# A decoder layer of three token mixers on one core: row sums of x taken from its transposed blocks, first loads issued behind casts, roots corrected on GpSimd

## The chip, the core and the metric

The kernel runs on one core of one Trainium2 chip. The metric is the device time of one execution in microseconds (us). Before the change the median of three runs is 323.5 us (323.33 to 324.22). The profile shows one execution of the program, taken by the hardware profiler. TensorE is called PE, VectorE DVE, ScalarE ACT, GpSimd POOL and SyncE SP; PEld is PE's weight load.

## What is computed

The input x has 256 rows (tokens) of 1024 float32 values; mem has 256 rows of the same width. In short form, as the reference has it:

```
h = rmsnorm(x, g_in);  z = h @ w_in                  # 8776 columns: q, k, v, gates, logits of three mixers
ya = moba_attention(rope(mq), rope(mk), mv)          # 8 heads of 64, causal
yb = dsa_attention(rope(dq), rope(dk), dv, rope(iq), rope(ik), iw)   # 64 keys chosen by an indexer
yc = cross_attention(xq, *split(rmsnorm(mem, g_mem) @ w_mem_kv))     # 4 heads of 128
u = sum over b of sigmoid(logits_b + b_merge) * ((y_b * silu(gate_b)) @ w_up_b)
out = rmsnorm(x + u @ w_out, g_final)
```

rmsnorm divides each row by the root of its mean square plus 1e-6. That factor of x (x_rstd) and of mem (m_rstd), one number per row, is what the change computes in another way.

## The kernel before, in words

**Products.** Every float32 matrix is split into a high part (a cast to fp32r on ACT) and a low part (the difference, on DVE), and a product is three matmuls: high x high, high x low, low x high. x and mem come transposed (xT, memT: 1024 features as 8 blocks of 128 partitions, 256 tokens each), are multiplied by g_in or g_mem while they are split (`split_act`, lines 180 to 191), and stay in SBUF. The row factors are applied after the product, where results leave PSUM.

**Steps.** All weights are cut into 100 steps of up to 512 KB (`plan.steps`); the list ORDER and the helpers `gemm...` set their order. Steps 0 to 7 take mv and mq in turn (mv's blocks 0 and 1, mq's 0 and 1, mv's 2 and 3, and so on), so that two steps use up one pair of xT's blocks. Then mk0, mk1, the indexer's i0, and the rest. The main loop (lines 984 to 1004) issues, for step s: the split of a pair of x's blocks (first four even steps), side work that was hung on s, the load of step s+6 (`load_weights`), the split of step s+3 (`split_weights`), the first half of the products of s, side work of s + 0.5, and the second half. Negative s is the run-up.

**What sets the order.** On PE and GpSimd the instructions stand in the order in which the program issues them. On DVE, ACT and SP the framework orders them, by program order as priority and by when it expects inputs and buffers to be free; `tc.issue_after(i)` keeps an instruction of the same engine behind i. A DMA is issued by SP or, where `queue=nc.scalar` is given, by ACT. Raw weights have four buffers (WRAW), so a load waits for the low part of the step four before it; split weights have five.

**The start.** SP issues x_first (xT's block 0 with gains and biases), w0's first block, xT's block 1, w0's second block, w1 in two halves, xT's blocks 2 and 3 and w2 (lines 171 to 175 and 969 to 973). `load_late` (lines 975 to 982) issues w3 and xT's blocks 4 and 5 on ACT behind the last cast of w0, and w4, w5 and xT's blocks 6 and 7 on SP. Meanwhile PE runs nine warm-up products of 128x128 (WARM, line 967).

**Roots.** `load_rows` (lines 887 to 892) loads x a second time, not transposed, in two loads of 128 rows (LOAD_ROWS = -2). `start_stats` (line 894, hung on step 6) squares the rows on ACT with an accumulated sum, and `rsqrt` (line 214) makes x_rstd: a scaling on DVE, a square root on ACT, a reciprocal and a Newton correction of four small operations on DVE (lines 220 to 223, 128x2 each). From x_rstd come `tab`, `rB` (its transposed form, two PE transposes at step 8, line 913) and all results scaled by row. For mem, `square_sum` (line 193) squares each pair of transposed blocks on ACT and adds the pairs up on DVE, and `row_sums` (line 203) sums over partitions with products with a column of ones; m_rstd and its transposes mB follow at steps 21.5 and 23.5. MEM gives the steps at which mem's four pairs are loaded (2, 7, 11, 15); each is split three steps later. xT's raw blocks and memT's share one buffer.

**Attention.** `attend` hangs each pair of heads of mixer A on two steps given in M_PAIRS: at s0 the scores (`self_scores`: PE, then a masked minimum on DVE, exponentials on ACT), half a step later their scaling on GpSimd (`self_scale`, line 616), at s1 the transposes of the probabilities (`self_transpose`: PE, a cast mph on ACT, the difference mpl on DVE), a step later the product with v (`self_values`, line 642, output mya). `idx_transpose` (line 443) turns the indexer's queries at steps 27 and 28 through PSUM banks of the kind "sc", of which there are two, used by scores too.

Of the kernel before, what the change touches and what calls it, by code (L numbers as in the profile page):

```python
# [58 lines left out]
SPLIT_AHEAD = 3  # L59
LOAD_AHEAD = 6  # L60
WRAW = 4
WARM = 9
HALVED = 2
ORDER = (
# [4 lines left out]
)  # L69
LOAD_ROWS = -2  # L70
X_STATS = 6

IDX = (27, 29, 33.5)

TURNS = (('mq', 8.5, 15.5), ('mk', 13.5, 20.5), ('dq', 27, 30), ('dk', 34, 37.5))

M_PAIRS = ((23, 25.5), (24, 27.5), (26.5, 29.5), (29.5, 31.5))
D_PAIRS = ((43.5, 47.5), (47.5, 49), (52, 53.5), (54.5, 55.5))
X_HEADS = (41.5, 44.5, 49, 50.5)
GATES = 59.5  # L80

MEM = (2, 7, 11, 15, 21.5)


def block_places(blocks, nk):
# [8 lines left out]
class Steps:  # L94
# [11 lines left out]
    def at(self, step, fn, *args):  # L106
        self.side[step].append((fn, args))
# [3 lines left out]
def hybrid_layer_kernel(  # L111
# [14 lines left out]
    nc = tc.nc  # L126
# [3 lines left out]
    work = ctx.enter_context(tc.tile_pool(name="work", bufs=2))  # L130
# [6 lines left out]
    at = plan.at  # L137
# [22 lines left out]
    acts = {}  # L160
# [19 lines left out]
    def split_act(raw, hi, lo, gcol, pair, nm):  # L180
        for j in range(2):
            k = 2 * pair + j
            g = x_first[:, S + gcol + k : S + gcol + k + 1]
            src = x_first[:, 0:S] if nm == "x" and k == 0 else raw[:, j, :]
            nc.scalar.activation(hi[:, k, :], src, AF.Copy, scale=g)
            nc.vector.scalar_tensor_tensor(
                lo[:, k, :], src, g, hi[:, k, :].bitcast(F32),
                op0=OP.mult, op1=OP.subtract,
            )
        if nm == "e":  # L190
            square_sum(raw, nm, pair)

    def square_sum(raw, nm, pair):

        sq = work.tile([P, 2, S], F32, name=f"{nm}sq{pair}", tag=("nat" if pair == 0 else "gate"),
                       bufs=3)
        nc.scalar.activation(sq, raw, AF.Square)
        if pair == 0:
            acts[nm, "sq"] = sq
        else:  # L200
            nc.vector.tensor_tensor(acts[nm, "sq"], acts[nm, "sq"], sq, op=OP.add)

    def row_sums(nm):

        ps = psum.tile([P, 512], F32, name=f"{nm}ss", tag="tp", bufs=1)
        for t in range(2):
            for j in range(2):
                nc.tensor.matmul(
                    ps[:, t : t + 1], acts[nm, "sq"][:, j, t * P : (t + 1) * P], ones[:, 0:1],
                    start=j == 0, stop=j == 1,  # L210
                )
        return ps[:, 0:2]

    def rsqrt(r, ss, nm):

        v, sd, e = (work.tile([P, 2], F32, name=f"{nm}n{i}", tag=f"n{i}") for i in range(3))
        nc.vector.tensor_scalar(v, ss, 1.0 / D, EPS, op0=OP.mult, op1=OP.add)
        nc.scalar.activation(sd, v, AF.Sqrt)
        nc.vector.reciprocal(r, sd)
        nc.vector.tensor_tensor(e, r, r, op=OP.mult)  # L220
        nc.vector.tensor_tensor(e, e, v, op=OP.mult)
        nc.vector.tensor_scalar(e, e, -0.5, 1.5, op0=OP.mult, op1=OP.add)
        nc.vector.tensor_tensor(r, r, e, op=OP.mult)


    loaded, halves = {}, {}
    last_hi = [None]

    def load_weights(s, j=None, queue=nc.sync):
        src, off, nk_all, n, k0, nk = plan.steps[s][0]  # L230
        if not j:
            loaded[s] = raws.tile([P, nk, n], F32, name=f"w{s}r", tag="wraw", bufs=WRAW)
        a, b = (0, nk) if j is None else (j, j + 1)
        v = bass.AP(
            tensor=src.tensor, offset=src.offset + off + (k0 + a) * n,
            ap=[[nk_all * n, P], [1, (b - a) * n]],
        )
        queue.dma_start(loaded[s][:, a:b, :].rearrange("p k n -> p (k n)"), v)

    def split_weights(s):  # L240
        raw = loaded.pop(s)
        shape = list(raw.shape)
        hi = ws.tile(shape, F32R, name=f"w{s}h", tag="whi")
        lo = ws.tile(shape, F32R, name=f"w{s}l", tag="wlo")
        part = 1 if s < HALVED + 2 else shape[1]
        for j in range(0, shape[1], part):
            ks = slice(j, j + part)
            last_hi[0] = nc.scalar.copy(hi[:, ks, :], raw[:, ks, :]).ins
            nc.vector.tensor_sub(lo[:, ks, :], raw[:, ks, :], hi[:, ks, :].bitcast(F32))
        halves[s] = (hi, lo)  # L250

# [191 lines left out]
    def idx_transpose(t):  # L443
# [4 lines left out]
                idx[nm] = keep.tile([P, 3 * P], F32, name=nm, tag=nm)  # L448
        tok = slice(t * P, (t + 1) * P)
        for j in range(2):  # L450
            tp = psum.tile([P, 4, P], F32R, name=f"iqt{t}{j}", tag="sc", bufs=2)
            for g in range(4):
                nc.tensor.transpose(tp[:, g, :], idx["qs", t][:, 4 * j + g, :], ident_r)
            nc.scalar.copy(idx["q"][j][:, :, tok], tp)
# [427 lines left out]
    attend("m", M_PAIRS, lambda: bias_c)  # L882
    attend("d", D_PAIRS, lambda: idx["sel"])

    x_rows = []

    def load_rows():
        for t in range(2):
            rows = keep.tile([P, 4, S], F32, name=f"x_rows{t}", tag=("khi", "klo")[t])
            rows = rows.rearrange("p a b -> p (a b)")  # L890
            nc.sync.dma_start(rows, x[t * P : (t + 1) * P, :])
            x_rows.append(rows)

    def start_stats():
        sums = work.tile([P, 2], F32, name="xss", tag="xss", bufs=1)
        for t in range(2):
            junk = work.tile([P, D], F32, name=f"xjunk{t}", tag="sw", bufs=1)
            nc.scalar.activation(junk, x_rows[t], AF.Square, accum_out=sums[:, t : t + 1])
        rsqrt(x_rstd, sums, "x")
        nc.vector.tensor_scalar_mul(xs_rstd, x_rstd, float(P**-0.5))  # L900
        nc.vector.tensor_copy(ident_r, ident)
        for t in range(2):
            nc.vector.tensor_scalar_mul(tab[:, t, :], tab0[:, t, :], x_rstd[:, t : t + 1])
# [11 lines left out]
            )  # L915
        nc.vector.tensor_copy(dst, tp[:, 0:S])

    at(LOAD_ROWS, load_rows)
    at(X_STATS, start_stats)
    at(X_STATS, make_bias)  # L920
    at(X_STATS + 2, rstd_rows, x_rstd, rB, "rB")
# [44 lines left out]
    warm = psum.tile([P, 512], F32, name="warm", tag="tp", bufs=1)  # L966
    for _ in range(WARM):
        nc.tensor.matmul(warm[:, 0:P], ones, ones, start=True, stop=True)  # L968
    first = [load_act(xT, 0, "x", 0)]
    load_weights(1, 0)  # L970
    load_weights(1, 1)
    first.append(load_act(xT, 0, "x", 1))
    load_weights(2)

    def load_late():

        with tc.issue_after(last_hi[0]):
# [91 lines left out]
```

## Time and profile before

| what | value |
|---|---|
| median of three runs | 323.5 us (323.33 to 324.22) |
| the profiled execution's own time | 324.77 us |
| its span, from the first to the last instruction | 323.0 us |
| moved by DMA | 59.45 MB, 184 GB/s over the span |

The profile counts as busy the time in which an engine has an instruction in it; matmuls are pipelined, so PE's busy share is high where matmuls follow each other, and its holes are what is to be looked for. In the timeline a row gives the start, the duration, engine, line, operation, output and inputs by the program's names, the shapes, how many were merged, and in brackets the idle time of the engine just before and what ended it. Lines such as L249 are lines of the kernel. A letter q behind an engine's name (SPq, ACTq) marks its sequencer, which issues DMAs.

### The profile page before, as it was taken

How to read it: one execution, taken by the hardware profiler on the slowest of the kernel's cores; microseconds unless marked ns; L12 is line 12 of the kernel's file. 1: busy time of each engine (PE TensorE's matmuls, PEld its weight loads, DVE VectorE, ACT ScalarE, POOL GpSimd, SP SyncE). 2: the span in 40 equal slices, each digit the busy share in tenths (PEclk: the TensorE clock that was granted, in tenths of full speed). 3: DMA queues.
4: the chain of work that ended last, by engine and by line, in shares of the span. 5: the costliest groups of instructions: out<-in, count | busy, mean ns of one | idle time of the engine just before them, and what ended most of it. 6: DMA issues, size and time to landing. Idle time of an engine off the chain costs nothing.

```text
span 323.0 us, 6395 instructions
## 1 busy us (share of the span) xinstructions
PE 313.0 (97%) x2442; PEld 297.4 (92%) x2442; DVE 252.1 (78%) x458; ACT 202.9 (63%) x357; POOL 41.9 (13%) x58
## 2 busy tenths in 40 slices
PE   8899999998999999999999999999999999999992
PEld 7699999988999989879999999999999999998882
DVE  3579999899799999988766759998466775677523
ACT  5599674687878545577666588756444546643434
POOL 0001000017202000010200235321000111014011
PEclk9999999999999999999999999999999999999999
DMA  6989886864644446574443434478765666655003
GB/s 202 379 293 333 269 269 194 265 240 124 214 130 127 138 130 210 182 246 131 146 132 117 146 94 162 136 220 302 211 193 189 190 188 205 182 156 188 2 0 130
DMA packets 18368, 59.45 MB, mean 184 GB/s; under 512 B 2209, under 2 KB 2465, under 8 KB 18337
## 3 DMA queue, kind: packets, MB, share of 16 engines
q1 hardware_dynamic: 17760, 57.73, 57.1%
q10 hardware_dynamic: 576, 1.31, 1.0%
q8 instruction: 19, 0.31, 0.5%
q14 instruction: 13, 0.10, 0.1%
HBM read 55.89 MB, written 1.05 MB: 176 GB/s over the span
## 4 chain that ended last, share of the span: by engine, by line
PE 70%; DVE 15%; DMA 5%; ACT 4%; issue 4%; SPq 0%; ACTq 0%; DVEq 0%
DMA w3r<-w_in 3%; DVE wk L498 2%; DMA w25r<-w_in 2%; DVE m L496 1%; PE o_0ps L255 1%; PE o_0ps L256 1%; PE o_0ps L254 1%; DMA w0r<-w_in 1%; PE dya L642 1%; PE i_0ps L280 1%; PE i_1ps L280 1%; PE mv_1ps L280 1%; PE mv_0ps L280 1%; DVE acc L487 1%; PE lg L480 1%
## 5 line engine op out<-in xcount | busy, mean ns | idle before, releaser
L747 POOL TENSOR_TENSOR u<-u,gt 128x512 f32<-128x512 f32 x7 | 9.9, 1411 | 76.7 <-DVE gt L744 76.7
L616 POOL TENSOR_SCALAR dpr<-dpr,dst 128x128 f32<-128x128 f32 (+1 forms) x16 | 6.6, 425 | 84.1 <-DVE dst L614 83.9
L616 POOL TENSOR_SCALAR mpr<-mpr,mst 128x128 f32<-128x128 f32 (+1 forms) x16 | 9.8, 629 | 56.3 <-DVE mst L614 56.3
L734 ACT ACTIVATE gt<-gt,x_first 128x256 f32<-128x256 f32 x24 | 10.9, 501 | 2.7 <-DVE gt L731 2.5
L606 ACT ACTIVATE dpr<-dms,dst 128x128 f32<-128x128 f32 (+1 forms) x16 | 7.1, 446 | 3.6 <-DVE dst L602 3.6
L788 ACT ACTIVATE junk<-xn 128x512 f32<-128x512 f32 (+1 forms) x5 | 2.7, 543 | 8.6 <-DVE xn L786 8.6
L606 ACT ACTIVATE mpr<-mms,mst 128x128 f32<-128x128 f32 (+1 forms) x16 | 7.1, 444 | 1.2 <-DVE mst L602 1.2
L664 ACT ACTIVATE xpr<-xsc,xst,xs_rstd 128x256 f32<-128x256 f32 x8 | 4.4, 560 | 3.4 <-DVE xst L660 3.4
L752 ACT CAST us<-u 128x512 fp32r<-128x512 f32 x4 | 2.5, 624 | 6.2 <-POOL u L747 4.9
L647 ACT COPY dyT<-dya 64x256 f32<-64x256 f32 x8 | 2.9, 367 | 4.2 <-PE dya L642 4.1
L484 ACT ACTIVATE rl<-lg 128x384 f32<-128x384 f32 x8 | 3.9, 485 | 2.7 <-PE lg L480 1.6
L487 DVE SCALAR_TENSOR_TENSOR acc<-rl,iw,acc 128x128 f32<-128x128 f32 (+1 forms) x14 | 5.4, 431 | 0.1
L480 PE MATMUL lg<-ikT,iqT 128*128 128x128 f32 (+1 forms) x32 | 5.1, 282 | 0.1
L968 PE MATMUL warm<-ones 128*128 128x128 f32 x18 | 4.0, 419 | 1.1 <-DVE eps_t L963 1.1
L602 DVE CUSTOM_DVE_ANT_0 mms<-msc,bias_c 128x128 f32<-128x128 f32 (+1 forms) x16 | 5.0, 350 | 0.0
L968 PEld LDWEIGHTS warm<-ones 128*128 128x128 f32 x18 | 3.9, 328 | 1.1 <-DVE eps_t L963 1.1
L648 DVE TENSOR_TENSOR dyT<-dyT,dya 64x256 f32<-64x256 f32 x8 | 3.3, 417 | 1.8 <-ACT dyT L647 1.7
L628 ACT CAST dph<-dtp 128x384 fp32r<-128x384 f32 x8 | 3.8, 479 | 1.4 <-PE dtp L627 1.3
L629 DVE TENSOR_TENSOR dpl<-dtp,dph 128x384 fp32r<-128x384 f32 x8 | 4.4, 553 | 0.4
L602 DVE CUSTOM_DVE_ANT_0 dms<-dsc,sel 128x128 f32<-128x128 f32 (+1 forms) x16 | 4.7, 352 | 0.0
L786 DVE TENSOR_TENSOR xn<-o_0ps,xn 128x512 f32<-128x512 f32 x2 | 1.4, 691 | 4.2 <-PE o_0ps L256 4.2
L498 DVE MATCH_REPLACE8 wk<-m,wk 128x128 f32<-128x128 f32 (+1 forms) x14 | 4.7, 342 | 0.0
(1296 smaller groups left out, 1541.9 us busy)
## 6 DMA issues: line engine op xcount, KB each, us to landing
x_rows<-x SPq DMA_DIRECT2D x2, 512.0 KB, 8.7
eT<-memT SPq DMA_DIRECT2D x4, 256.0 KB, 4.6
xn<-x SPq DMA_DIRECT2D x2, 512.0 KB, 5.5
w0r<-w_in SPq DMA_DIRECT2D x2, 256.0 KB, 3.3
w1r<-w_in SPq DMA_DIRECT2D x2, 256.0 KB, 4.9
xT<-xT SPq DMA_DIRECT2D x2, 256.0 KB, 7.1
w2r<-w_in SPq DMA_DIRECT2D x1, 512.0 KB, 7.3
w3r<-w_in ACTq DMA_DIRECT2D x1, 512.0 KB, 8.7
```

What stands on the lines that cost most here:

```text
L280: nc.tensor.matmul(accs[nm][t][:, :n], a[p](k, slice(t * P, (t + 1) * P)), w[q][:, half, :], start=k + i == 0, stop=k + i == nk + 1,)
L480: nc.tensor.matmul(lg[:, c : c + n], q[:, q0:q1], idx["k"][:, j, 0:n], start=j == 0, stop=j == 1)
L487: nc.vector.scalar_tensor_tensor(acc[:, c], rl[:, c], iw[:, t, g : g + 1], (bias_c if g == 0 else acc)[:, c], op0=OP.mult, op1=OP.add,)
L498: nc.vector.match_replace(out=wk[:, c], in_to_replace=m8[t], in_values=src[:, c], imm_value=TAKEN)
L602: nc.vector.tensor_tensor_reduce(out=ms[:, c], in0=sc[:, c], in1=bias()[:, c], op0=OP.add, op1=OP.min, scale=-(HD**-0.5), scalar=3e38, acc ...
L606: big["last_exp"] = nc.scalar.activation(pr[:, c], ms[:, c], AF.Exp, bias=st[:, t : t + 1], scale=-1.0, accum_out=st[:, 2 + t : 3 + t],)
L616: nc.gpsimd.tensor_scalar(pr[:, c], pr[:, c], st[:, 4 + t : 5 + t], 1.0, op0=OP.mult, op1=OP.mult)
L629: nc.vector.tensor_sub(pl, tp[:, 0 : 3 * P], ph.bitcast(F32))
L664: big["last_exp"] = nc.scalar.activation(pr3[:, t, :], sc[:, t, :], AF.Exp, bias=st[:, t : t + 1], scale=xs_rstd[:, t : t + 1], accum_out= ...
L734: nc.scalar.activation(gt[:, f, :], gt[:, f, :], AF.Sigmoid, bias=x_first[:, j : j + 1])
L747: adder.tensor_tensor(u, u, gt, op=OP.add)
L968: nc.tensor.matmul(warm[:, 0:P], ones, ones, start=True, stop=True)
```

## The change

- **Row sums of x.** The second load of x and the squares over its rows are gone. `square_sum` now also runs for x, on its four pairs of transposed blocks, at steps 1, 2, 3 and 4 (X_SQUARES), and folds the two blocks of the pair sum into one at the end, so that `row_sums` needs one product per 128 tokens instead of two, for x and for mem. x's row sums stand at step 6.
- **Loads.** `load_late` is called twice, behind each cast of w1's two halves: first xT's third pair and then w3 on ACT, then w4 on ACT, w5 on SP and behind it xT's last pair. The two tables cst and tabT are kept behind the last load that was issued before step 1.
- **First cast.** The first cast of w0 is done in two halves of its columns, one on ACT and one on DVE.
- **Roots.** The four correcting operations of `rsqrt` run on GpSimd.
- **Places.** One warm-up product less; the second pair of mixer A at step 24.5 instead of 24; mem's first pair loaded at step 5 instead of 2; the transposes of the indexer's queries go through PSUM banks of the kind "mm", of which there are four.

```
-WARM = 9
+WARM = 8
-LOAD_ROWS = -2
+X_SQUARES = (1, 2, 3, 4)
-M_PAIRS = ((23, 25.5), (24, 27.5), (26.5, 29.5), (29.5, 31.5))
+M_PAIRS = ((23, 25.5), (24.5, 27.5), (26.5, 29.5), (29.5, 31.5))
-MEM = (2, 7, 11, 15, 21.5)
+MEM = (5, 7, 11, 15, 21.5)
...
-        nc.scalar.activation(sq, raw, AF.Square)
+        raw = acts[nm, "raw"]
+        if nm == "x" and pair == 0:
+            nc.scalar.activation(sq[:, 0, :], x_first[:, 0:S], AF.Square)
+            nc.scalar.activation(sq[:, 1, :], raw[:, 1, :], AF.Square)
+        else:
+            nc.scalar.activation(sq, raw[:, 2 * pair : 2 * pair + 2, :], AF.Square)
         if pair == 0:
             acts[nm, "sq"] = sq
-        else:
-            nc.vector.tensor_tensor(acts[nm, "sq"], acts[nm, "sq"], sq, op=OP.add)
+            return
+        total = acts[nm, "sq"]
+        nc.vector.tensor_tensor(total, total, sq, op=OP.add)
+        if pair == 3:
+            nc.vector.tensor_tensor(total[:, 0, :], total[:, 0, :], total[:, 1, :], op=OP.add)
...
-            for j in range(2):
-                nc.tensor.matmul(
-                    ps[:, t : t + 1], acts[nm, "sq"][:, j, t * P : (t + 1) * P], ones[:, 0:1],
-                    start=j == 0, stop=j == 1,
-                )
+            nc.tensor.matmul(
+                ps[:, t : t + 1], acts[nm, "sq"][:, 0, t * P : (t + 1) * P], ones[:, 0:1],
+                start=True, stop=True,
+            )
...
-        nc.vector.tensor_tensor(e, r, r, op=OP.mult)
-        nc.vector.tensor_tensor(e, e, v, op=OP.mult)
-        nc.vector.tensor_scalar(e, e, -0.5, 1.5, op0=OP.mult, op1=OP.add)
-        nc.vector.tensor_tensor(r, r, e, op=OP.mult)
+        nc.gpsimd.tensor_tensor(e, r, r, op=OP.mult)
+        nc.gpsimd.tensor_tensor(e, e, v, op=OP.mult)
+        nc.gpsimd.tensor_scalar(e, e, -0.5, 1.5, op0=OP.mult, op1=OP.add)
+        nc.gpsimd.tensor_tensor(r, r, e, op=OP.mult)
...
-            last_hi[0] = nc.scalar.copy(hi[:, ks, :], raw[:, ks, :]).ins
+            cols = slice(0, shape[2] // 2 if s + j == 0 else shape[2])
+            last_hi[0] = nc.scalar.copy(hi[:, ks, cols], raw[:, ks, cols]).ins
+            if s + j == 0:
+                cols = slice(shape[2] // 2, shape[2])
+                nc.vector.tensor_copy(hi[:, ks, cols], raw[:, ks, cols])
+            if s == 1:
+                load_late(j)
...
-            tp = psum.tile([P, 4, P], F32R, name=f"iqt{t}{j}", tag="sc", bufs=2)
+            tp = psum.tile([P, 4, P], F32R, name=f"iqt{t}{j}", tag="mm", bufs=4)
...
-        sums = work.tile([P, 2], F32, name="xss", tag="xss", bufs=1)
-        for t in range(2):
-            junk = work.tile([P, D], F32, name=f"xjunk{t}", tag="sw", bufs=1)
-            nc.scalar.activation(junk, x_rows[t], AF.Square, accum_out=sums[:, t : t + 1])
-        rsqrt(x_rstd, sums, "x")
+        rsqrt(x_rstd, row_sums("x"), "x")
...
-    at(LOAD_ROWS, load_rows)
+    for pair, s0 in enumerate(X_SQUARES):
+        at(s0, square_sum, "x", pair)
...
-    def load_late():
+    def load_late(j):
         with tc.issue_after(last_hi[0]):
-            load_weights(3, queue=nc.scalar)
-            first.append(load_act(xT, 0, "x", 2, nc.scalar))
-        load_weights(4)
-        load_weights(5)
-        first.append(load_act(xT, 0, "x", 3))
+            if j == 0:
+                first.append(load_act(xT, 0, "x", 2, nc.scalar))
+                load_weights(3, queue=nc.scalar)
+            else:
+                load_weights(4, queue=nc.scalar)
+                load_weights(5)
+                with tc.issue_after(last_load[0]):
+                    first.append(load_act(xT, 0, "x", 3))
...
+        if s == 1:
+            mark = last_load[:]
         if s == 4:
-            nc.sync.dma_start(cst, consts[:, 0:512])
-            nc.sync.dma_start(tabT.rearrange("p t c -> p (t c)"), consts[:, 512:1024])
+            with tc.issue_after(mark[0]):
+                nc.sync.dma_start(cst, consts[:, 0:512])
+                nc.sync.dma_start(tabT.rearrange("p t c -> p (t c)"), consts[:, 512:1024])
```

## Rows read from the trace of the kernel before

**Rows 1.** The page: busy time of each engine, and the granted clock in 40 slices.
```profile
PE 313.0 (97%) x2442; PEld 297.4 (92%) x2442; DVE 252.1 (78%) x458; ACT 202.9 (63%) x357; POOL 41.9 (13%) x58
...
PEclk9999999999999999999999999999999999999999
```

**Rows 2.** Busy time by stretch: length, busy us of each engine, clock, DMA share, GB/s.
```profile
2.00:9.00 7.00, 6.79 (x31) 5.51 (x30) 2.96 (x5) 3.41 (x8) 0.00 (x0) 1.00 0.85 265
...
5.01:18.74 13.73, 12.82 (x72) 10.01 (x72) 8.46 (x14) 8.25 (x16) 0.00 (x0) 1.00 0.98 356
18.74:61.90 43.16, 43.16 (x343) 42.08 (x342) 39.99 (x64) 31.44 (x50) 1.25 (x2) 1.00 0.84 263
30.00:60.00 30.00, 30.00 (x255) 30.00 (x255) 29.09 (x44) 19.55 (x33) 0.00 (x0) 1.00 0.80 239
61.90:80.00 18.10, 16.69 (x141) 15.29 (x141) 17.58 (x54) 14.68 (x33) 6.74 (x11) 1.00 0.59 191
```

**Rows 3.** PE's waits: line, whom it waited for, us in total, times, longest.
```profile
PE mya L642 <- DVE mpl L629: 1.0, 1, 1.0
PE mBt L913 <- DVE m_rstd L223: 0.4, 1, 0.4
```

**Rows 4.** PE's timeline at the start: warm-up, first products of steps 0, 1, 4, 6.
```profile
1.05 4.05 PE L968 MATMUL warm<-ones 128*128 128x128 f32 x18 [1.05 <-DVE eps_t L963]
...
5.01 0.50 PE L280 MATMUL mv_0ps<-w0h,xhi 128*128 128x512 f32 x1
...
8.18 0.29 PE L254 MATMUL mq_0ps<-xhi,w1h 128*128 128x256 f32 x1
...
18.86 0.40 PE L280 MATMUL mv_0ps<-w4h,xhi 128*128 128x512 f32 x1
...
24.45 0.40 PE L280 MATMUL mv_0ps<-w6h,xhi 128*128 128x512 f32 x1
```

**Rows 5.** ACT's timeline at the start: casts of weights and the issue of w3.
```profile
4.34 0.62 ACT L248 CAST w0h<-w0r 128x512 fp32r<-128x512 f32 x1 [0.89 <-DMA w0r<-w_in]
...
6.05 1.31 ACTq L238 DMA_DIRECT2D w3r<-w_in  x1
7.41 0.62 ACT L248 CAST w1h<-w1r 128x512 fp32r<-128x512 f32 x1 [1.17 <-DMA w1r<-w_in]
...
11.32 1.14 ACT L248 CAST w2h<-w2r 128x512 fp32r<-128x512 f32 x2 [0.58 <-DMA w2r<-w_in]
14.76 1.14 ACT L248 CAST w3h<-w3r 128x512 fp32r<-128x512 f32 x2 [2.30 <-DMA w3r<-w_in]
```

**Rows 6.** The page's DMA issues: tile, count, KB each, median us from issue to landing.
```profile
x_rows<-x SPq DMA_DIRECT2D x2, 512.0 KB, 8.7
```

**Rows 7.** Instructions grouped by line and shape: busy us, mean ns of one, idle before.
```profile
L898 ACT ACTIVATE xjunk<-x_rows 128x1024 f32<-128x1024 f32 x2 | 2.1, 1052 | 0.0
...
L516 ACT COPY mqT<-mq_0ps 128x256 f32<-128x256 f32 x2 | 0.7, 372 | 0.0
...
L201 DVE TENSOR_TENSOR esq<-esq,esq 128x512 f32<-128x512 f32 x3 | 2.0, 678 | 0.0
```

**Rows 8.** Timeline: first and last step of mem's root on DVE; x's transposes on PE.
```profile
63.81 0.17 DVE L219 RECIPROCAL m_rstd<-en 128x2 f32<-128x2 f32 x1 [0.32 <-ACT en L218]
...
66.92 0.15 DVE L223 TENSOR_TENSOR m_rstd<-m_rstd,en 128x2 f32<-128x2 f32 x1
...
30.05 0.38 PE L913 MATMUL rBt<-cst,x_rstd 128*128 128x128 f32 x2
```

**Rows 9.** GpSimd's scalings of 128x128: two from 75.1 us, one from 69 us.
```profile
L616 POOL TENSOR_SCALAR mpr<-mpr,mst 128x128 f32<-128x128 f32 x2 | 2.8, 1422 | 0.0
...
L616 POOL TENSOR_SCALAR mpr<-mpr,mst 128x128 f32<-128x128 f32 x1 | 0.4, 372 | 40.4 <-DVE mst L614 40.4
```

**Rows 10.** Timeline: the cast before mpl on ACT, the second pair's scalings on GpSimd.
```profile
75.98 0.46 ACT L628 CAST mph<-mtp 128x384 fp32r<-128x384 f32 x1
...
75.02 5.53 POOL L616 TENSOR_SCALAR mpr<-mpr,mst 128x128 f32<-128x128 f32 x6
```

More of the change, by code (lines that the diff above doesn't have):

```diff
@@ L190, in split_act, with square_sum @@
         if nm == "e":
-            square_sum(raw, nm, pair)
-    def square_sum(raw, nm, pair):
+            square_sum(nm, pair)
+    def square_sum(nm, pair):
         sq = work.tile([P, 2, S], F32, name=f"{nm}sq{pair}", tag=("nat" if pair == 0 else "gate"),
                        bufs=3)
-        nc.scalar.activation(sq, raw, AF.Square)
+        raw = acts[nm, "raw"]
[4 more added lines that the diff above has]
+            nc.scalar.activation(sq, raw[:, 2 * pair : 2 * pair + 2, :], AF.Square)
         if pair == 0:
             acts[nm, "sq"] = sq
-        else:
-            nc.vector.tensor_tensor(acts[nm, "sq"], acts[nm, "sq"], sq, op=OP.add)
+            return
[3 more added lines that the diff above has]
+            nc.vector.tensor_tensor(total[:, 0, :], total[:, 0, :], total[:, 1, :], op=OP.add)
     def row_sums(nm):
@@ L219, in rsqrt @@
         nc.vector.reciprocal(r, sd)
-        nc.vector.tensor_tensor(e, r, r, op=OP.mult)
-        nc.vector.tensor_tensor(e, e, v, op=OP.mult)
-        nc.vector.tensor_scalar(e, e, -0.5, 1.5, op0=OP.mult, op1=OP.add)
-        nc.vector.tensor_tensor(r, r, e, op=OP.mult)
+        nc.gpsimd.tensor_tensor(e, r, r, op=OP.mult)
+        nc.gpsimd.tensor_tensor(e, e, v, op=OP.mult)
+        nc.gpsimd.tensor_scalar(e, e, -0.5, 1.5, op0=OP.mult, op1=OP.add)
+        nc.gpsimd.tensor_tensor(r, r, e, op=OP.mult)
     loaded, halves = {}, {}
-    last_hi = [None]
+    last_hi, last_load = [None], [None]
     def load_weights(s, j=None, queue=nc.sync):
@@ L237, in load_weights @@
         )
-        queue.dma_start(loaded[s][:, a:b, :].rearrange("p k n -> p (k n)"), v)
+        last_load[0] = queue.dma_start(
+            loaded[s][:, a:b, :].rearrange("p k n -> p (k n)"), v
+        ).ins
     def split_weights(s):
@@ L883, in hybrid_layer_kernel @@
     attend("d", D_PAIRS, lambda: idx["sel"])
-    x_rows = []
-    def load_rows():
-        for t in range(2):
[L889 to L892, printed above, removed]
-    def start_stats():
-        sums = work.tile([P, 2], F32, name="xss", tag="xss", bufs=1)
-        for t in range(2):
-            junk = work.tile([P, D], F32, name=f"xjunk{t}", tag="sw", bufs=1)
-            nc.scalar.activation(junk, x_rows[t], AF.Square, accum_out=sums[:, t : t + 1])
-        rsqrt(x_rstd, sums, "x")
+    def start_stats():
+        rsqrt(x_rstd, row_sums("x"), "x")
         nc.vector.tensor_scalar_mul(xs_rstd, x_rstd, float(P**-0.5))
@@ L959, in hybrid_layer_kernel @@
     at(end["u01"], load_tail)
+    first = [load_act(xT, 0, "x", 0)]
     nc.vector.memset(ones, 1.0)
@@ L968, in hybrid_layer_kernel @@
         nc.tensor.matmul(warm[:, 0:P], ones, ones, start=True, stop=True)
-    first = [load_act(xT, 0, "x", 0)]
     load_weights(1, 0)
@@ L996, in hybrid_layer_kernel @@
             split_weights(s + SPLIT_AHEAD)
-            if s + SPLIT_AHEAD == 0:
-                load_late()
         if s >= 0:
```

## The prediction

> **What bounds the kernel now.** I read the page first: TensorE (PE) is busy 97% of the span and VectorE (DVE) 78%, GpSimd (POOL) 13%; the granted clock is full in all 40 slices, that is 2.4 GHz [rows 1], so the clock is no term of the sum. A busy PE is not an unbroken PE, so next came the table by stretch [rows 2]. Between 18.74 and 61.90 us PE is busy for all of 43.16 us; there only less matmul work would help, and the change removes none. What can be won lies where PE has holes: from 5.01 to 18.74 us, where the 16 DMA engines are 98% busy, and from 61.90 to 80 us, where DVE is busy 17.58 of 18.10 us. The list of PE's waits [rows 3] names the two that make the second stretch's 1.41 idle us: 0.97 for the first pair's probabilities (mpl) and 0.44 for the memory's root (m_rstd).
>
> The start is read from PE's timeline [rows 4]. Undisturbed, two steps take 24.45 - 18.86 = 5.59 us, 2.80 each. Steps 1 to 3 take 18.86 - 8.18 = 10.68 us, where 8.39 would do: 2.29 us are lost. Their cause stands in ScalarE's (ACT) timeline [rows 5]: the casts wait for w1r, w2r and w3r. w3r is issued at 6.05 and cast only at 14.76, because xT's third part, w4, two loads of x's rows and w5 are issued around it and share the same engines; the loads of x's rows take 8.7 us each to land [rows 6].
>
> **First product.** It starts at 5.01 [rows 4], when the cast of w0's first block ends (4.34 + 0.62 [rows 5]); the warm-up ends there too (4.05 us from 1.05 [rows 4]). The change splits the cast: a 128x256 copy takes 0.37 on ACT [rows 7], so it ends at about 4.72; one warm-up product of nine less takes 0.45 off. The start moves by about 0.26. Step 0's second block waits for its own load as now, and its order of products leaves room for an end 0.26 earlier. Term: **-0.26 us**; bounds 0 and -0.45.
>
> **Loads behind casts, x's rows gone.** Two loads of 512 KB leave the queue [rows 6], at 356 GB/s [rows 2] 2.9 us of all the DMA engines, and two issues leave SP. xT's third part and w3 are now issued behind w1's first cast, so at 7.0 to 7.4 instead of up to 6.05, w4 behind its second cast, w5 and xT's last part after that on SP. What must land before step 2 (x_first, w0, two parts of xT, w1, w2) is 2.07 MB by shape; at 265 GB/s, the rate of 2 to 9 us [rows 2], it is there at about 9.7 if nothing shares; w2 is cast at 11.32 now. w3 makes it 2.84 MB, at 356 GB/s 2.2 us later: 12 to 13 with some sharing, and PE asks for it at about 14. So w3 stops being late. What is late next is ACT: three issues stand between its casts, and w3r's issue held it for 1.31 us [rows 5], so w1's second cast would start near 8.7, no earlier than now, and the lo parts still come one DVE operation later. I leave 0.9 of the 2.29 us: **-1.4 us**; bounds -0.3 (each issue takes 1.31, and step 2 starts hardly earlier) and -2.29 (the issues hold nothing).
>
> **Row sums from the blocks.** Out go two squares over whole rows, 2 x 1.05 us of ACT [rows 7] between 18 and 21 us; in come three squares of 128x512 at 0.62 (the cast of that size, [rows 5]) and one in two halves of 0.37, 2.6 us, at steps 1 to 4. DVE gets three sums of 0.68 [rows 7], two folds and a copy of half that size (0.4 each, an estimate from it): 3.2 us, while eight small operations of 0.15 [rows 8] leave it. Most lies before 20 us, where DVE is busy 8.46 of 13.73 us [rows 2]; without that cover it would be 2 us more in the chain of rival 1. On PE the sums of x cost what those of mem save, as each needs half the products. But x's sums now stand in PE's order at step 6, at 24.45 - 1.66 = 22.8. The last block of x, loaded behind w5, I expect squared by 19 and folded by 20.5: no wait. Term: **0**; bounds 0 and +0.5.
>
> **Roots on GpSimd.** The memory's root takes from 63.81 to 67.07 on DVE [rows 8], since each 0.15 us step gets its turn behind a subtraction of 1.2 us, and PE waits 0.44 for it. No two-input GpSimd operation on two columns is in the trace. The nearest rows are 128x128 scalings, of which one took 0.37 and two 1.42 each where DVE ran w28l to w30l [rows 9]. Four operations would take 1.5 to 5.7 us, against 3.26. DVE's order now would let two of them meet w25l and w26l and two meet operations that read PSUM: about 3.1. Term: **-0.1 us**; bounds -0.44 and the loss of rival 2. For x the reciprocal comes at best at 23.8 (sums 0.4, root and reciprocal 0.6), the four end at 26.9, and PE transposes them at step 8, 30.05 - 1.66 + 0.4 = 28.8 [rows 8]: covered.
>
> The Trainium skill (SBUF — State Buffer, Who interferes with whom) says that a VectorE instruction with two SBUF inputs and a GpSimd instruction that reads SBUF shut each other out for a whole instruction. By that rule the 1.42 beside 0.37 is this lock, the trace agrees, and the sum would be rival 2's.
>
> **Second pair half a step later.** PE waits 0.97 us in mya [rows 3], because ACT casts mph only at 75.98 [rows 10], behind the second pair's exponentials. Half a step is 1.4 us. If the pair falls behind mph, mpl is there in time and the wait goes; if the order on ACT and DVE stays, nothing does. The pair's own scalings end at 80.5 [rows 10] and its transposes come at step 27.5, after 83 us, so a loss is excluded. Between 0 and -0.97 I take **-0.5 us**.
>
> The rest costs nothing. mem's first part is issued three steps later, and its buffer is x's, so it waits for x's last reader now too; three weight loads pass it on SP. The tables cst and tabT may go out right after w6, 0.5 MB that nothing near needs to wait for. The transposes of iq move to another bank; none of PE's seven waits is theirs.
>
> Sum: -0.26 - 1.4 - 0 - 0.1 - 0.5 = **-2.26 us**. The profiled execution took 324.77 (span 323.0), 1.27 above the median of 323.5; less 2.26 it would be 322.5, and the median 321.2. The 1.66 us of the first two terms are kept from 18.86 to 61.9, where PE has no hole, if DVE keeps pace.
>
> **Rivals.**
> 1. **DVE gives it back.** Between 30 and 60 us DVE is busy 29.09 of 30 us [rows 2]. If that chain doesn't start earlier, PE arrives 1.66 us earlier at m_rstd and mpl and waits as much longer; only 0.2 is left: 323.3. Against it: the chain hangs on casts that hang on the same late loads, and 2.1 us of ACT leave just ahead of it.
> 2. **GpSimd's four steps each wait out a DVE operation** (the other side). At 1.42 each, from 62.3 (63.98 - 1.66), m_rstd is there at 68.0; PE asks now at about 66.7, then at 65.0, and waits 3.0 us instead of 0.44. x's root ends at 23.8 + 5.7 = 29.5 for 28.8: 0.7 more. 2.5 + 0.7 - 1.66 = +1.6, the pair unmoved: 325.1. It makes the kernel slower by over 0.3% from 1.35 us per step on. For it: the rows of 1.42 [rows 9]. Against: the row of 0.37, and a 128x2 operation is shorter.
> 3. **Both late waits go and no load is late**: -0.26 - 2.29 - 0.44 - 0.97 = -3.96: 319.5.
> 4. **It doesn't do what it says**: the order on DVE, ACT and SP is the framework's. If x's last block comes late, PE waits at step 6; if the issues hold ACT, the second term is -0.3: 322.3 to 323.
>
> **How the numbers follow.** Forecast 0.50, rival 1 0.16, rival 2 0.11, rival 3 0.17, rival 4 0.06. The likeliest time is 321.2, its own range 320.2 to 322.4. About 0.3% (0.97 us) is what a measurement of this kernel can tell from no change. Faster by more (under 322.53): the forecast, rival 3 and most of rival 4, 0.71; within it: rival 1 and the rest of 4, 0.18; slower: 0.11. The range reaches to rival 3's time and just past rival 1's, 319.3 to 323.6, and leaves out rival 2 and little below.
>
> **What would show it.** Right: PE's first product at about 4.75, step 4 at 17.2 instead of 18.86, no wait for w3r, m_rstd some 3 us after its reciprocal, a shorter wait in mya. Wrong: w1's second cast held by issues on ACT; GpSimd operations on two columns of over 1 us; a longer wait at mBt, or a new one at rBt or for x's sums; waits at 62 to 80 us that grow by what the start won.

## The result, and the profile after

The changed kernel takes 327.96 us (median of four executions, 327.7 to 330.25), the kernel before beside it 323.41 (322.72 to 324.22): a ratio of 1.0135, 95% interval 1.0098 to 1.0173. It is slower, by 4.55 us; the forecast was 321.2 and its range ended at 323.6. The profiled executions are 2.9 us apart (327.7 and 324.77; spans 325.9 and 323.0), since the one of before lay 1.4 above its median and the one after 0.3 below. The traces explain these 2.9.

The page of the changed kernel, against [rows 1]: shares alike, and the clock full in all slices but the last of 40.

```profile
PE 316.8 (97%) x2440; PEld 302.6 (93%) x2440; DVE 254.3 (78%) x456; ACT 203.0 (62%) x358; POOL 45.5 (14%) x66
...
PEclk9999999999999999999999999999999999999998
```

By stretch (length, busy us of each engine, clock, DMA share, GB/s), against [rows 2]: the DMA engines are a little freer at the start, and VectorE is as full as before from 30 to 60 us.

```profile
5.01:18.74 13.73, 13.26 (x75) 10.75 (x76) 9.71 (x16) 9.98 (x19) 0.00 (x0) 1.00 0.93 324
30.00:60.00 30.00, 30.00 (x251) 30.00 (x250) 29.54 (x47) 19.51 (x34) 0.24 (x2) 1.00 0.73 221
```

PE's waits (line, whom it waited for, us in total, times, longest), against [rows 3]: m_rstd is gone, mya shorter, and a small one is new, at x's sums (xss); xpt, mv_0ps and the indexer's product lg (0.1 before) wait 0.1 to 0.2 longer. By this list the change worked.

```profile
PE mya L657 <- DVE mpl L644: 0.6, 1, 0.6
PE xpt L699 <- ACT xpr L689: 0.5, 1, 0.5
PE mv_0ps L295 <- ACT w2h L258: 0.4, 1, 0.4
PE lg L495 <- DVE mst L617: 0.2, 1, 0.2
PE xss L215 <- DVE xsq L209: 0.2, 1, 0.2
```

The start of PE's timeline (start, duration), against [rows 4], then ACT's, against [rows 5]:

```profile
1.05 3.78 PE L972 MATMUL warm<-ones 128*128 128x128 f32 x16 [1.05 <-DVE eps_t L967]
4.91 0.74 PE L295 MATMUL mv_0ps<-w0h,xhi 128*128 128x512 f32 x1
...
8.64 0.28 PE L269 MATMUL mq_0ps<-xhi,w1h 128*128 128x256 f32 x1
...
18.10 0.40 PE L295 MATMUL mv_0ps<-w4h,xhi 128*128 128x512 f32 x1
...
24.12 0.58 PE L215 MATMUL xss<-ones,xsq 128*128 128x1 f32 x4 [0.24 <-DVE xsq L209]
24.55 0.48 PE L295 MATMUL mv_0ps<-w6h,xhi 128*128 128x512 f32 x1
```

```profile
4.45 0.41 ACT L258 CAST w0h<-w0r 128x256 fp32r<-128x256 f32 x1 [0.68 <-DMA w0r<-w_in]
...
6.21 0.62 ACT L258 CAST w0h<-w0r 128x512 fp32r<-128x512 f32 x1 [0.57 <-DMA w0r<-w_in]
...
7.26 0.44 ACTq L245 DMA_DIRECT2D w3r<-w_in  x1
8.73 0.62 ACT L258 CAST w1h<-w1r 128x512 fp32r<-128x512 f32 x1 [1.28 <-DMA w1r<-w_in]
...
11.42 1.14 ACT L258 CAST w2h<-w2r 128x512 fp32r<-128x512 f32 x2 [0.61 <-DMA w2r<-w_in]
13.29 1.14 ACT L258 CAST w3h<-w3r 128x512 fp32r<-128x512 f32 x2 [0.73 <-DMA w3r<-w_in]
```

Step 4 starts at 18.10, 0.76 earlier than before, where 1.66 was forecast: w3's wait is down from 2.30 to 0.73, and its issue took 0.44, not 1.31, but w0's second block, w1 and w2 are still waited for. Step 6 is 0.10 later than before: PE reaches x's sums at 23.88 and waits for VectorE's fold, which stands behind w7's subtraction (VectorE's timeline):

```profile
22.41 1.23 DVE L264 TENSOR_TENSOR w7l<-w7r,w7h 128x1024 fp32r<-128x1024 f32 x1
23.55 0.42 DVE L209 TENSOR_TENSOR xsq<-xsq 128x256 f32<-128x256 f32 x1
```

Where the 2.9 us come from shows only when steps are timed from first product to first product. Step 30 starts at 96.75 before and 96.45 after (-0.30); from there to step 92 it is 197.60 and 201.28 (+3.68); the rest is 28.61 and 28.17 (-0.44). Between 30 and 92 the waits hardly differ (0.24 more at xpt, 0.11 less at dya); most products start later after the one ahead of them. The first products of steps 60 and 70, a stretch without a wait, before and then after:

```profile
204.75 0.28 PE L254 MATMUL l00ps<-xhi,w60h 128*128 128x256 f32 x1
...
232.75 0.28 PE L254 MATMUL u01ps<-mgyh,w70h 128*128 128x256 f32 x1
```

```profile
205.57 0.28 PE L269 MATMUL l00ps<-xhi,w60h 128*128 128x256 f32 x1
...
234.37 0.28 PE L269 MATMUL u01ps<-mgyh,w70h 128*128 128x256 f32 x1
```

Ten steps of 24 products of 256 columns take 28.00 us before and 28.80 after: 116.7 and 120.0 ns a product. The row's duration, 0.28 in both, doesn't show this. Products of 512 columns went the other way, 233.3 to 226.7 ns (steps 36 to 37).

### The profile page after: what moved, and what is told of

It is laid out like the page before. It is cut to its first block, busy times and chain, and to the rows that moved or that the text cites. A ratio compares the mean times of both kernels' runs of the same rounds, so it can differ in the third digit from the quotient of the medians.

```text
span 325.9 us, 6401 instructions
## 1 busy us (share of the span) xinstructions
PE 316.8 (97%) x2440; PEld 302.6 (93%) x2440; DVE 254.3 (78%) x456; ACT 203.0 (62%) x358; POOL 45.5 (14%) x66
## 4 chain that ended last, share of the span: by engine, by line
PE 69%; DVE 15%; DMA 6%; issue 3%; ACT 3%; POOL 2%; SPq 0%; ACTq 0%; DVEq 0%
DMA w3r<-w_in 2%; DMA w7r<-w_in 2%; PE i_0ps L295 2%; PE i_1ps L295 2%; POOL mpr L631 1%; DVE wk L513 1%; DMA w0r<-w_in 1%; PE o_0ps L270 1%; PE o_0ps L269 1%; PE o_0ps L271 1%; DVE m L511 1%; PE dya L657 1%; DMA w42r<-w_kv 1%; PE dtp L642 1%; PE o_1ps L271 1%
## 5 line engine op out<-in xcount | busy, mean ns | idle before, releaser
L631 POOL TENSOR_SCALAR dpr<-dpr,dst 128x128 f32<-128x128 f32 (+1 forms) x16 | 7.6, 490 | 85.2 <-DVE dst L629 84.7
L807 POOL TENSOR_TENSOR xn<-xn,gf 128x512 f32<-128x512 f32 x2 | 2.6, 1296 | 15.7 <-ACT junk L803 15.7
```

Source lines behind the costliest of these rows:

```text
L631: nc.gpsimd.tensor_scalar(pr[:, c], pr[:, c], st[:, 4 + t : 5 + t], 1.0, op0=OP.mult, op1=OP.mult)
```

## The experiments

**What sets the rate.** The clock is the same. What differs for every product is where its operands lie. The change drops the tile xss, 32 bytes a partition, from a pool that is laid out ahead of x, mem and all later operands, while the weights' halves stay: in the compiled program x's high part lies at byte 138272 of a partition before and 138240 after, w0's at 52224 in both. Three runs put a tile back or add one, and only the size ([P, 2] is 32 bytes, [P, 16] is 64) and the kernel differ; a fourth repeats the changed kernel as it is:

```
     def start_stats():
+        pad = work.tile([P, 2], F32, name="pad", tag="pad", bufs=1)
+        nc.gpsimd.memset(pad, 0.0)
```

> The changed kernel with a tile of two columns (32 bytes a partition in the pool) put back where x's sums (xss) had stood, and one GpSimd memset of it, so that x, mem and all that lies behind them in SBUF stand again at an odd multiple of 32 bytes. Theory (addresses): PE's products of 256 columns start 116.7 ns after each other again and those of 512 columns 233.3 ns, steps take 2.80 us; 1823 products of 256 columns get 3.33 ns each back (6.1 us), 216 of 512 columns lose 6.6 ns each (1.4 us): 4.6 us less, about 323.3 us. Rival A (the order of PE's instructions, or the PSUM banks): 120 and 226.7 ns stay, 327.9 us. Rival B (that chip on that day): this kernel and the changed one unaltered come out alike, whatever the rate.

> The kernel before with the same tile of 32 bytes added, so that x, mem and all behind them move by 32 bytes to an even multiple, as in the changed kernel, and nothing else changes but one GpSimd memset. Theory (addresses): 120 ns per product of 256 columns and 226.7 per product of 512, steps of 2.88 us, some 4.6 us slower than before: 328 us. Rival A (order of PE's instructions, PSUM banks): 116.7 and 233.3 ns stay, 323.5 us. Rival B: as before unaltered.

> The changed kernel with a tile of 64 bytes instead of 32 in that place: everything behind it moves, but stays at an even multiple of 32 bytes. Theory (addresses, by multiples of 32): no change, 120 and 226.7 ns, 327.9 us. If any shift at all repairs it (the neighbours of single tiles matter), or the added memset does, then 116.7 ns and about 323.3 us.

> The changed kernel unaltered, beside the others on the same chip. Theory (addresses) and rival A: 120 and 226.7 ns, 327.9 us. Rival B (that chip on that day): 116.7 and 233.3 ns, 323 us.

Five more sizes followed, and one run in which the tile stands in the first pool (`const.tile`), so that x and the weights move together:

> The changed kernel with 96 bytes added where xss had stood. The runs so far: a shift of 0 gave 120.0 ns per product of 256 columns in an undisturbed step, 32 bytes gave 116.7, 64 bytes 117.8 (113.3 in six steps near the start), whichever kernel it was. Theory (the distance between the operands' addresses sets the rate, with a period of 128 bytes): a steady rate of its own, one of 113.3 to 120 ns; by symmetry with 32 bytes 116.7 ns, and then 323.5 to 324.5 us. Rival (each program has a rate of its own, for no reason of address): any rate, changing from step to step.

> The changed kernel with 128 bytes added there. Theory (period of 128 bytes): exactly as the changed kernel without a pad, 120.0 ns per product of 256 columns, 226.7 per product of 512, about 328 us. Rival (a longer period, or no rule of address): another rate, 113.3 to 117.8 ns, and 322 to 325 us.

> The changed kernel with 32 bytes added in the first pool, ahead of the weights too: x, mem and the weights' halves all move together, and x stands where the pad of 32 bytes alone had put it. If the distance between the two operands of a product counts: 120.0 ns and 226.7 ns stay, about 328 us. If the address of x (or of what stands behind it) alone counts: 116.7 and 233.3 ns, 324.5 us.

> The changed kernel with 160 bytes added where xss had stood. So far the distance between x's and the weights' addresses, counted from the changed kernel's own, gave per product of 256 columns in an undisturbed step: 0: 120.0 ns, 32: 116.7, 64: 117.8 or 113.3, 96: 120.2, 128: 118.7; moving both operands by 32 left 120.0. Theory (the distance sets the rate, with a period above 128 bytes): a steady rate of its own between 113.3 and 120.2 ns; no size is forecast. Rival (period of 128 after all, 128 having been disturbed): 116.7 ns and 324.5 us.

> The changed kernel with 192 bytes added there. Theory (the distance sets the rate, with a period above 128 bytes): a rate of its own between 113.3 and 120.2 ns; by symmetry with 64 in a period of 256, 113.3 to 117.8 ns and 318 to 325 us. Rival (period of 128): as 64 bytes, 117.8 ns, 325 us.

> The changed kernel with 256 bytes added there. Theory with a period of 256 bytes: as the changed kernel without a pad, 120.0 and 226.7 ns, 328 us. With a longer period: another rate, 113.3 to 118.7 ns, 318 to 327 us.

Distance is x's address less the weights', what is left over from multiples of 256 bytes; ns are means over steps 60 to 69 (256 columns) and step 36 (512), from one trace of each kernel.

| distance | kernels | ns, 256 | ns, 512 | ratio to before, 95% |
|---|---|---|---|---|
| 0 | after | 120.0 | 226.7 | 1.0135 (1.0098 to 1.0173) |
| 0 | after again (one execution, 328.71 us) | 120.0 | 226.7 | |
| 0 | after, all moved by 32 | 120.0 | 226.7 | 1.0133 (1.0103 to 1.0164) |
| 0 | after + 256 | 120.0 | 226.7 | 1.0145 (1.0114 to 1.0177) |
| 32 | before | 116.7 | 233.3 | 1 |
| 32 | after + 32 | 116.7 | 233.3 | 1.0031 (1.0004 to 1.0057) |
| 64 | before + 32 | 117.8 | 233.3 | 1.0053 (1.0031 to 1.0075) |
| 64 | after + 64 | 117.8 | 233.3 | 1.0050 (1.0030 to 1.0071) |
| 96 | after + 96 | 120.0 | 234.3 | 1.0166 (1.0137 to 1.0195) |
| 128 | after + 128 | 118.7 | 232.6 | 1.0109 (1.0083 to 1.0135) |
| 160 | after + 160 | 118.7 | 233.3 | 1.0086 (1.0060 to 1.0112) |
| 192 | after + 192 | 117.8 | 233.3 | 1.0032 (1.0013 to 1.0051) |

Where the distance is equal, the rate in these steps is, in whichever kernel; moving both operands changes nothing, moving one does; 256 bytes bring 120.0 back. So the distance between the operands sets the rate in these steps, and 32 bytes put back take the loss from 1.35% to 0.31%. My first rule, odd or even multiples of 32 bytes, fell: the kernel before with 32 bytes more lost 1.4 us (325.2 against 323.76), not 4.6, and the pad of 64 didn't leave the changed kernel at 327.9 but at 325.11. A period of 128 bytes fell too. Why a distance has its rate is open.

A pad also moves the operands against whatever other engines and transfers touch, so it must be asked whether PE loses time to them. The trace of the changed kernel says no: all 815 intervals between starts in steps 58 to 91 are 120 ns, the 65 in which VectorE, ScalarE and GpSimd are idle throughout and the 112 in which no DMA packet is in flight among them. One such stretch, as busy time (PE, PEld, then three idle engines) and as starts of PE:

```profile
288.60:289.21 0.61, 0.61 (x7) 0.61 (x6) 0.00 (x0) 0.00 (x0) 0.00 (x0) 1.00 0.42 161
```

```profile
288.61 0.28 PE L271 MATMUL u12ps<-dgyh,w88l 128*128 128x256 f32 x1
288.73 0.28 PE L269 MATMUL u12ps<-dgyh,w88h 128*128 128x256 f32 x1
288.85 0.28 PE L270 MATMUL u12ps<-dgyl,w88h 128*128 128x256 f32 x1
```

The Trainium skill (SBUF — State Buffer, Who interferes with whom) has PE's read of the moving operand and its weight load on two independent ports and lets PE wait on no one. The 815 equal intervals agree that no engine holds PE up, but two operands of PE's own products are not indifferent to each other: 113.3 to 120.0 ns by their distance.

**Two rhythms at one distance.** In the changed kernel at 192 bytes steps 9 to 11 and 17 to 19 ran at 113.3 ns and steps 58 to 91 at 117.8; at 64 bytes steps 9 to 11 ran at 113.3, but at 117.8 in the kernel before at the same 64. (At 160, too, steps 17 to 19 had 117.4 and the later ones 118.7.) So a few extra products, called kicks, were put between the steps:

```
+KICKS = {60: 8, 64: 16, 68: 32, 72: 64, 76: 96, 80: 128, 84: 192, 88: 256}
...
             w = halves.pop(s)
+            kick(s)
```

A kick is one product of x's high part with KICKS[s] of its own columns, into a bank that nothing reads.

> The changed kernel with the pad of 64 bytes (there a product of 256 columns took 117.8 ns in every step from 58 to 91, but 113.3 in steps 8 to 11), with one extra product into a bank that nothing reads at the start of eight of these steps: 8 columns wide at step 60, 16 at 64, 32 at 68, 64 at 72, 96 at 76, 128 at 80, 192 at 84, 256 at 88. Theory (at this distance two rhythms are stable, and which one runs is set by how the stream of products was last interrupted): after some of the eight the following four steps run at 113.3 ns (2.72 us a step), after others at 117.8 (2.83 us). Rival (the rhythm belongs to the operands of a step): 117.8 ns throughout, whatever stands between the steps.

> The same eight extra products in the changed kernel with the pad of 192 bytes (113.3 ns in steps 9 to 20, 117.8 from 58 to 91). Theory: as for 64 bytes, some of the eight leave 113.3 ns behind them. Rival: 117.8 ns throughout.

At 64 bytes 117.8 ns stayed after all eight: nothing there speaks against the rival. At 192 bytes the four steps behind each extra product ran at

| columns | 8 | 16 | 32 | 64 | 96 | 128 | 192 | 256 |
|---|---|---|---|---|---|---|---|---|
| ns | 113.3 | 117.8 | 113.3 | 113.3 | 113.3 | 117.8 | 113.3 | 117.8 |

with the same operands as without. PE's timeline of that kernel at step 60 shows the whole interruption:

```profile
203.80 0.17 PE L998 MATMUL kick<-xhi 128*128 128x8 f32 x1
203.83 0.36 PE L270 MATMUL l00ps<-xhi,w60h 128*128 128x256 f32 x1
```

It took 323.19 us beside 324.95 for the kernel before, one execution each.

**The version that beats both, and the change at equal rates.** `KICKS = {58: 8}` alone, in the changed kernel with 192 bytes and in the kernel before with 160, which puts x at the same address:

> The changed kernel with the pad of 192 bytes and one extra product of 8 columns at the start of step 58, where nothing after it breaks the stream up to step 91. Theory (the interruption chooses the rhythm and it holds until the next one): steps 59 to 91 run at 113.3 ns, 2.72 us instead of 2.83, so 33 x 0.11 = 3.6 us less, 0.1 back for the extra product; against 324.68 us with the pad alone about 321.2 us, under the kernel before. Rival (the rhythm falls back by itself): 117.8 ns return after some steps, 323 to 324.7 us.

> The kernel before with x put at the same address (160 bytes added) and the same extra product at step 58, so that the two kernels run their products at like rates and differ in the change alone. Theory (at equal rates the change is worth nothing: what it wins by 18 us it pays at x's sums, m_rstd and lg): within 0.3% of the changed kernel so treated, 320.5 to 322 us. Rival (the forecast's own sum): 2.3 us slower than it. If the extra product falls at another phase of the stream here, steps 59 to 91 stay at 117.8 ns, and the comparison is made on the time up to step 58.

Measured 320.98 us (ratio 0.9904, 0.9885 to 0.9923; 321.2 was expected) and 320.16 us (0.9888, 0.9865 to 0.9910): both beat the kernel before by about 1%, and so the changed one by 2%. Steps 59 to 91 take 2.72 us each in both, to the end. The intervals overlap, and the changed kernel's median is the longer by 0.8: at equal rates the change wins nothing that these runs show. The two traces show how that comes about. PE's waits and the first products of steps 6 and 30, in the changed kernel so treated:

```profile
PE xss L216 <- DVE xsq L210: 1.2, 1, 1.2
PE mBt L918 <- POOL m_rstd L231: 1.1, 1, 1.1
...
PE lg L496 <- DVE mst L618: 0.7, 1, 0.7
```

```profile
24.91 0.48 PE L296 MATMUL mv_0ps<-w6h,xhi 128*128 128x512 f32 x1
...
96.12 0.73 PE L496 MATMUL lg<-ikT,iqT 128*128 128x128 f32 x4 [0.68 <-DVE mst L618]
96.69 0.28 PE L270 MATMUL xk_0ps<-ehi,w30h 128*128 128x256 f32 x1
```

and in the kernel before so treated:

```profile
PE mBt L916 <- DVE m_rstd L224: 1.4, 1, 1.4
PE mya L643 <- DVE mpl L630: 1.2, 1, 1.2
```

```profile
23.21 0.40 PE L281 MATMUL mv_0ps<-w6h,xhi 128*128 128x512 f32 x1
...
96.21 0.73 PE L481 MATMUL lg<-ikT,iqT 128*128 128x128 f32 x4
96.78 0.29 PE L255 MATMUL xk_0ps<-ehi,w30h 128*128 128x256 f32 x1
```

Both reach step 4 alike (17.58 and 17.61; nothing of the start's gain is seen in this pair). The kernel before leads by 1.7 us at step 6, where the changed one waits for x's sums; the changed one leads by 1.5 at step 27 (81.11 against 82.57), after the other's longer waits for m_rstd and mpl; at step 30 both stand level, and from 31 on no step differs by more than 0.05. Of the lead of 1.5, 0.7 goes as a wait at lg, the rest in the steps just ahead of it.

**What paces lg.** Three runs took VectorE's work out, by having ScalarE write the low parts of some steps as plain copies (these kernels leave the subtraction out): steps 17 and 19, then 32 and 33, then all four.

```
-            nc.vector.tensor_sub(lo[:, ks, :], raw[:, ks, :], hi[:, ks, :].bitcast(F32))
+            if s in (17, 19):
+                nc.scalar.copy(lo[:, ks, :], raw[:, ks, :])
+            else:
+                nc.vector.tensor_sub(lo[:, ks, :], raw[:, ks, :], hi[:, ks, :].bitcast(F32))
```

> The changed kernel with the pad of 32 bytes (324.49 us), and the lo parts of w17 and w19 written by ScalarE as a plain copy of the loaded weights, not by VectorE as a difference: 2 x 1.22 us less of VectorE between 47 and 53 us, 2 x 1.05 us more of ScalarE, which has gaps of 2 to 4 us there. Part of the computation is thereby replaced (two steps' lo parts). Theory (VectorE, which runs without a break from 30 to 96 us, paces the arrival at PE's product lg at 96.25 us, and gives back what PE won before): lg starts up to 2 us earlier, the waits for m_rstd (1.7) and lg (0.5) shrink, and the time falls by 1 to 2 us, to 322.5 to 323.5 us. Rival (the start's gain is lost elsewhere, on PE, ScalarE or a DMA): lg stays at 96.2 us and the time at 324.5 us.

Measured 324.43 us, against 324.49: the median didn't move, though step 30 came 0.63 us earlier in the profiled execution (96.18). The theory's 1 to 2 us were not there: in VectorE's timeline the 2.4 us turned into waits for ScalarE's casts (1.45 at w20, 0.66 at w26, 0.51 at w27), and PE waited 0.6 at lg still. Nor was VectorE without a break, as the theory had it: in the pad-32 run it was busy 61.97 of the 66.20 us from 30 to 96.2. So VectorE's work at 47 to 53 us counts little in the time. The 0.63 us is no proof of the opposite: one kernel's step 30 can differ by more from execution to execution (below).

> The changed kernel with the pad of 192 bytes and one extra product (320.98 us; there VectorE runs without a break from 86.3 us on, PE waits 0.7 us at lg, which starts at 96.1), and the lo parts of w32 and w33 written by ScalarE as plain copies of the loaded weights (part of the computation is thereby replaced): 2 x 1.21 us less of VectorE between 87.7 and 93.1 us. Theory (VectorE's work between 84 and 96 us sets when lg starts): PE's wait at lg goes, step 30 starts 0.6 to 0.8 us earlier, at 95.9 to 96.1 us, the time is 320.2 to 320.4. Rival (lg hangs on PE's and ScalarE's own work, or on the load that dqT waits for): lg's wait stays over 0.5 us, step 30 at 96.7, 321.0 us.

> The same with the lo parts of w17 and w19 written by ScalarE as well (part of the computation is thereby replaced), as in the run with the pad of 32 bytes, where that moved step 30 from 96.81 to 96.18 us in the profiled execution but left the median at 324.4. Theory: the two reliefs add where VectorE paces both stretches: step 30 at 95.0 to 95.6 us, the time 319.5 to 320 us. Rival (the first relief buys nothing that a median shows): as with w32 and w33 alone.

Measured 320.09 and 319.63 us (0.9892, 0.9875 to 0.9910, and 0.9874, 0.9854 to 0.9895). With w32 and w33 off VectorE the wait at lg is gone, and step 30 comes at 95.19, 1.5 us earlier than in the kernel it is compared with (96.69):

```profile
94.66 0.69 PE L499 MATMUL lg<-ikT,iqT 128*128 128x128 f32 x4
```

Taking w17 and w19 off as well left step 30 at 95.21, as the rival had it (the theory's 95.0 to 95.6 holds it too). Three traces of kernels that are alike up to step 58 (192 bytes, with no, one or eight extra products) have step 30 at 97.31, 96.69 and 95.92, and waits at lg of 0.68, 0.68 and 0.11; the two without w32 and w33 are earlier than all of them and have no wait. Beside the kernel before, the gain went from 2.94 us to 3.42 and 3.88, and each interval overlaps the next. So where PE does wait at lg, it is VectorE's work that it waits for (in the kernel with the one extra product VectorE is busy 9.64 of the 9.70 us from 86.3 to 96.0), and a lead that PE has won earlier is lost there; how much of this the time gets back is not settled by these runs.

**The roots.** One run undid that part alone, all four steps, with the pad of 32 bytes:

```
-        nc.gpsimd.tensor_tensor(e, r, r, op=OP.mult)
+        nc.vector.tensor_tensor(e, r, r, op=OP.mult)
...
```

> The changed kernel with the pad of 32 bytes, and the roots' corrections back on VectorE; against the pad of 32 bytes alone (324.49 us; there two of the four GpSimd steps for mem's root took 1.13 and 1.15 us beside the subtractions for w26l and w27l, the other two 0.19, and PE waited 1.7 us for m_rstd). Theory (GpSimd's steps wait out VectorE's subtractions): on VectorE the four steps take their turns behind w25l to w27l as before, m_rstd comes 3.1 to 3.7 us after its reciprocal, PE's wait for it is 1.5 to 2.0 us, no shorter, and the time stays within 0.3 us. Rival (it is GpSimd that costs the wait): the wait falls to 0.5 and the time by 1 us to 323.5 us; mya's wait may come back with it.

Measured 324.8 us, against 324.49: no change, as the theory said, but not for its reason. m_rstd was done 2.5 us after its reciprocal's start, since three of the four steps found VectorE free, and PE's wait for it was gone; but then PE waited 0.9 us for mpl instead, and 0.6 at lg (0.5 before). How GpSimd pays is plain in the pad-32 run, in which PE waits 1.7 us for m_rstd. GpSimd's timeline, then VectorE's:

```profile
64.95 1.13 POOL L227 TENSOR_TENSOR en<-m_rstd 128x2 f32<-128x2 f32 x1 [36.39 <-DVE m_rstd L226]
66.15 1.15 POOL L228 TENSOR_TENSOR en<-en,en 128x2 f32<-128x2 f32 x1
67.39 0.19 POOL L229 TENSOR_SCALAR en<-en 128x2 f32<-128x2 f32 x1
```

```profile
64.80 1.23 DVE L264 TENSOR_TENSOR w26l<-w26r,w26h 128x1024 fp32r<-128x1024 f32 x1
66.02 1.23 DVE L264 TENSOR_TENSOR w27l<-w27r,w27h 128x1024 fp32r<-128x1024 f32 x1
```

The first two steps end within 0.06 us of the subtractions they met (66.03 and 67.25); alone a step takes 0.19. The Trainium skill (SBUF — State Buffer, Who interferes with whom) speaks of a lock that shuts one of the two engines out while the other's instruction runs; these rows agree with it. In the changed kernel itself VectorE happened to stand idle for 0.91 us there, three steps took 0.20 and only the last met w26's subtraction:

```profile
64.69 0.19 POOL L229 TENSOR_SCALAR en<-en 128x2 f32<-128x2 f32 x1
64.97 1.27 POOL L230 TENSOR_TENSOR m_rstd<-m_rstd,en 128x2 f32<-128x2 f32 x1
```

## Why the prediction was wrong

The step that failed is the one with no term: "there only less matmul work would help, and the change removes none". It took a product's price as given wherever PE has no hole. The price changed, by 3.3 ns for products of 256 columns, 3.7 us from step 30 to 92. The edit that did it, a tile of two columns that is no longer needed, was costed nowhere; it stood among the row sums, whose term was 0. The runs with pads show that cause: the same 32 bytes put back bring 116.7 ns back.

That leaves the forecast's own sum of -2.26, which failed too. Its terms are measured by the pad-32 run, in which products run as before (116.7 ns), step by step against the kernel before:

| term | forecast | measured | read from |
|---|---|---|---|
| first product and loads | -1.66 | -0.92 | step 4: 18.86 to 17.94 |
| row sums, x less mem | 0 | +0.37 | step 4 to step 8 +0.81, within step 21 -0.44 |
| roots on GpSimd | -0.1 | +1.27 | step 22 -0.55 to step 25 +0.72 |
| second pair | -0.5 | -1.04 | step 25 +0.72 to step 27 -0.32 |
| lg | none | +0.38 | step 27 -0.32 to step 30 +0.06 |
| sum | -2.26 | +0.06 | step 30: 96.75 to 96.81; spans 323.0 and 323.1 |

This is one trace beside one. Step 4 comes at 17.41 to 18.55 us in the 17 traces of the changed kernel and its variants, and at 18.86, 19.05 and 17.61 in the three of the kernel before and its variants, so the size of the first term is not shown, and the others are sizes in this pair.

- **First product, loads.** The first product came at 4.91 in the changed kernel and 4.73 here: -0.10 and -0.28, for -0.26. Loads were right in kind (w3 is no longer the one that is late) and, in this pair, half in size (-0.64 for -1.4): w0's second block, w1 and w2 are waited for as before.
- **Row sums.** In the changed kernel the last squares were done at 20.5, not 19, and the fold at 23.97, not 20.5: VectorE did w6 and w7 between. PE's wait at step 6 was 0.1 to 1.4 us from trace to trace, and none in one, where "no wait" was forecast.
- **Roots and second pair.** Rival 2's mechanism happened, for one or two of the four steps, at 1.13 to 1.27 us rather than the 1.42 of [rows 9]; where VectorE was free the price was 0.19 to 0.20. From the reciprocal's start to m_rstd's end [rows 8] has 3.26 us; the changed kernel took 2.35 and the pad-32 run 3.15. Where PE waits longer for m_rstd it finds mpl ready, and the reverse: 1.27 and -1.04 are one wait in two places, as the run with the roots on VectorE shows.
- **Rival 1** was right that VectorE takes back what the start wins, wrong about where: at x's sums, where PE waits for VectorE's fold, and at lg, where the kernel before waits only 0.1 us. I read the stretch from 62 to 80 us and stopped there.

So without the rate the kernel would have stood level with before by the traces, and measured 324.49 beside 323.76 (1.0031, 1.0004 to 1.0057): not faster either, and past the end of the range. The rate made it clearly slower. The chance of slower, 0.11, stood on rival 2 alone.

## What to carry to other kernels

Before explaining a changed time by waits, compare the start-to-start distance of the same products in a stretch without waits: a tile added or dropped elsewhere can move every later tile and with it the rate of most products. When the rate differs, shift the operands back by a pad before judging the change. A gain ahead of an engine that works without a break can be lost again where PE next waits for that engine; look for the first later product that waits on it, and follow the wait list past the stretch where the change acts.

## What was not expected of the hardware

- Products of 256 columns start every 113.3, 116.7, 117.8, 118.7 or 120.0 ns by the distance between their operands' addresses, at the same granted clock; at a distance of 0 all 815 intervals of steps 58 to 91 were 120 ns, whether other engines worked or not. The distance of 0, which with 96 is the worst for 256 columns, is the best for 512 (226.7 ns against 232.6 to 234.3).
- At a distance of 192 bytes two rates hold in one kernel, and one product of 8 columns changed 117.8 ns to 113.3 for the 33 steps behind it. At 64 bytes, where 113.3 also occurs, none of eight widths did so in the one execution tried. What selects the rate is open.
- A GpSimd operation on 128x2 values took 0.19 us alone and 1.13 to 1.27 beside a VectorE subtraction of 1.23 us.
